# RMS normalisation on one core: statistics one group ahead, the first load in parts, and three large transfers split by partitions

## The chip, the cores and the metric

The kernel runs on one core of one Trainium2 chip. The metric is the device time of one execution in microseconds (us), and lower is better. Quoted times are medians of several executions. The span that a profile shows, from the first to the last instruction, is 1.7 to 1.8 us shorter than the time of the same execution. All timed runs here had a granted clock of 1.0.

## The reference

```python
batch, seq, dim = 16, 1024, 512          # x: float32, gamma: ones
rms = np.sqrt(np.mean(x ** 2, axis=-1, keepdims=True) + 1e-5)
return (x / rms * gamma).astype(np.float32)
```

Each row of 512 numbers is divided by its own root mean square. 33.5 MB are read and 33.5 MB are written, and every row is independent of the others.

## The kernel before

The 16,384 rows are cut into four tiles. A tile gives each of the 128 partitions R = 32 consecutive rows (64 KB), 8.39 MB in all. Three slots in SBUF hold the tiles; tile 3 goes into slot 0 after tile 0 has been stored. SyncE issues all large transfers on one queue.

```python
xv = xf.rearrange("(t p r) d -> t p r d", p=P, r=R)
slots = [const.tile([P, R, D], fp32, name=f"slot{i}") for i in range(3)]

def load(t, slot, r0, r1):
    nc.sync.dma_start(out=slots[slot][:, r0:r1], in_=xv[t][:, r0:r1])

def store(t, slot, r0, r1):
    nc.sync.dma_start(out=ov[t][:, r0:r1], in_=slots[slot][:, r0:r1])

load(0, 0, 0, 16)
load(0, 0, 16, 32)
load(1, 1, 0, 32)
# ... gamma is loaded and spread over the partitions ...

def compute(slot, r0, r1):
    for g in range(r0, r1, G):            # G = 8 rows
        # ... odd groups: Square on ACT into PSUM, tensor_reduce on DVE
        # ... even groups: Square with accum_out on ACT, row by row
        # ... rms = Sqrt(ss / D + eps) on ACT, rstd = reciprocal on DVE
        for r in range(G):                # slot = slot * rstd * gamma on DVE
            nc.vector.scalar_tensor_tensor(...)

compute(0, 0, 8)
store(0, 0, 0, 1); load(2, 2, 0, 16)      # cut: three one-row stores alternate
# ...                                     # with the loads of tile 2
compute(0, 8, 32)
store(0, 0, 3, 32)
# ... tile 1 is stored in two halves of 16 rows, load(3, 0, ...) twice ...
compute(2, 0, 32)
store(2, 2, 0, 32)
compute(0, 0, 16); store(3, 0, 0, 16)
compute(0, 16, 32); store(3, 0, 16, 32)
```

## Time and profile before

| | before |
|---|---|
| time, median (6 runs beside the changed kernel) | 162.05 us |
| span of the profiled execution | 161.0 us |
| DMA queue 1, share of 16 engines' span | 97.4% |
| packet time per DMA engine (sum over 16, divided) | 156.9 us |
| DVE busy | 123.3 us |
| ACT busy | 79.9 us |

The profiled execution of the kernel before took 162.76 us, a little longer than the six timed runs (161.86 to 162.15). So differences between two single traces that are below 1 us are read with care.

These are lines of the profile's page of the kernel before. The rows of digits are busy tenths in 40 slices of about 4 us. Then come the DMA queue, the chain of waits by engine, and two instruction groups (busy us, mean ns, then the engine's idle time before them and what ended it).

```profile
span 161.0 us, 414 instructions
...
DVE  0101909999999509999999999998999999997000
ACT  3007999930490999999500933003998960000000
...
DMA  7999999969798999999699999999999699699993
GB/s 253 399 407 497 399 423 489 521 293 489 326 466 356 466 403 501 460 472 443 297 480 407 415 480 407 407 489 407 407 497 521 277 505 521 269 489 407 407 391 138
...
q1 hardware_dynamic: 2448, 67.11, 97.4%
...
DVE 70%; ACT 12%; DMA 8%; issue 2%; DVEq 0%
...
L78 ACT ACTIVATE sq_scratch<-slot 128x512 f32<-128x512 f32 x64 | 40.1, 627 | 14.4 <-DMA slot<-in_x_dram 13.1
L73 DVE TENSOR_REDUCE ss<-sq 128x4 f32<-128x2048 f32 x16 | 36.1, 2273 | 10.3 <-ACT sq L72 10.2
```

How to read it: the chain of waits names DVE for 70% of the span, yet the DMA row is nearly full from end to end. The queue's own line settles it. The 16 DMA engines spend 97.4% of the span on packets, so no rearrangement of compute can save more than the few per cent that are left. The engines' end times in the trace agree: the last packet ends at 159.65 us, and the rest of the span is completion and the closing barrier.

The windows view gives the rate in three stretches: tile 1's load, tile 0's large store and tile 2's store, each from the last landing of the transfer before it to its own last landing. The last two columns are the DMA share and GB/s.

```profile
22.70:42.40 19.70, 0.00 (x0) 0.00 (x0) 18.45 (x26) 11.08 (x23) 0.00 (x0) 1.00 0.96 407
63.90:82.10 18.20, 0.00 (x0) 0.00 (x0) 18.20 (x29) 14.63 (x37) 0.00 (x0) 1.00 0.97 418
121.30:140.60 19.30, 0.00 (x0) 0.00 (x0) 19.04 (x28) 9.98 (x21) 0.00 (x0) 1.00 1.00 433
```

The engines are full (0.96 to 1.00) and move 407 to 433 GB/s. A view counts a packet where it starts, so a single slice can read above or below the rate of a long window (the slices above, without the first and the last, go from 269 to 521 GB/s); a long window is safer.

The timeline shows when the last store was issued:

```profile
145.87 2.07 DVE L87 SCALAR_TENSOR_TENSOR slot<-slot,rstd,gamma_b 128x512 f32<-128x512 f32 x3
147.97 0.33 SPq L45 DMA_DIRECT2D out_dram<-slot  x1
```

### The profile page before, as it was taken

How to read it: one execution, taken by the hardware profiler on the slowest of the kernel's cores; microseconds unless marked ns; L12 is line 12 of the kernel's file. 1: busy time of each engine (PE TensorE's matmuls, PEld its weight loads, DVE VectorE, ACT ScalarE, POOL GpSimd, SP SyncE). 2: the span in 40 equal slices, each digit the busy share in tenths (PEclk: the TensorE clock that was granted, in tenths of full speed). 3: DMA queues.
4: the chain of work that ended last, by engine and by line, in shares of the span. 5: the costliest groups of instructions: out<-in, count | busy, mean ns of one | idle time of the engine just before them, and what ended most of it. 6: DMA issues, size and time to landing. Idle time of an engine off the chain costs nothing.

```text
span 161.0 us, 414 instructions
## 1 busy us (share of the span) xinstructions
PE 2.0 (1%) x2; PEld 0.5 (0%) x2; DVE 123.3 (77%) x163; ACT 79.9 (50%) x162; POOL 0.2 (0%) x4
## 2 busy tenths in 40 slices
PE   3100000000000000000000000000000000000000
PEld 1000000000000000000000000000000000000000
DVE  0101909999999509999999999998999999997000
ACT  3007999930490999999500933003998960000000
POOL 0000000000000000000000000000000000000000
DMA  7999999969798999999699999999999699699993
GB/s 253 399 407 497 399 423 489 521 293 489 326 466 356 466 403 501 460 472 443 297 480 407 415 480 407 407 489 407 407 497 521 277 505 521 269 489 407 407 391 138
DMA packets 2452, 67.13 MB, mean 417 GB/s; under 512 B 273, under 2 KB 273, under 8 KB 658
## 3 DMA queue, kind: packets, MB, share of 16 engines
q1 hardware_dynamic: 2448, 67.11, 97.4%
q14 instruction: 2, 0.02, 0.0%
q10 hardware_dynamic: 2, 0.00, 0.0%
HBM read 33.56 MB, written 33.55 MB: 417 GB/s over the span
## 4 chain that ended last, share of the span: by engine, by line
DVE 70%; ACT 12%; DMA 8%; issue 2%; DVEq 0%
DVE slot L87 51%; DVE ss L73 18%; DMA slot<-in_x_dram 8%; ACT sq_scratch L78 6%; ACT sq L72 4%; DVE rstd L85 1%; ACT L84 1%; ACT rms L84 1%; DVEq L142 0%
## 5 line engine op out<-in xcount | busy, mean ns | idle before, releaser
L87 DVE SCALAR_TENSOR_TENSOR slot<-slot,rstd,gamma_b 128x512 f32<-128x512 f32 x128 | 85.8, 747 | 0.1
L78 ACT ACTIVATE sq_scratch<-slot 128x512 f32<-128x512 f32 x64 | 40.1, 627 | 14.4 <-DMA slot<-in_x_dram 13.1
L73 DVE TENSOR_REDUCE ss<-sq 128x4 f32<-128x2048 f32 x16 | 36.1, 2273 | 10.3 <-ACT sq L72 10.2
L72 ACT ACTIVATE sq<-slot 128x2048 f32<-128x2048 f32 x16 | 29.8, 1865 | 13.9 <-DVE ss L73 13.9
L84 ACT ACTIVATE rms<-ss,eps_t 128x8 f32<-128x8 f32 x16 | 4.5, 298 | 27.9 <-DVE ss L73 27.7
L78 ACT ACTIVATION_READ_ACCUMULATOR sq_scratch<-slot 128x1 f32 x64 | 12.1, 189 | 0.0
L85 DVE RECIPROCAL rstd<-rms 128x8 f32<-128x8 f32 x16 | 2.9, 193 | 9.8 <-ACT rms L84 9.8
L58 DVE COPY gamma_b<-sq 128x512 f32<-128x512 f32 x1 | 0.7, 691 | 3.6 <-PE sq L56 3.6
L56 PE MATMUL sq<-gamma_row,ones_col 1*128 1x512 f32 x2 | 2.0, 1122 | 2.5 <-DMA gamma_row<-in_gamma_dram 2.5
L78 ACT ACT_TABLE_LOAD x1 | 1.3, 1283 | 1.3 <-PEq L131 1.3
L84 ACT ACT_TABLE_LOAD x1 | 1.3, 1283 | 0.0
L54 DVE MEMSET ones_col<- 1x128 f32 x1 | 0.2, 165 | 0.8 <-PEq L131 0.8
L56 PEld LDWEIGHTS sq<-gamma_row,ones_col 1*128 1x128 f32 x2 | 0.5, 305 | 2.5 <-issue 2.5
L131 POOL MEMSET const-bfloat16-1.0<- 128x1 bf16 x1 | 0.1, 103 | 0.0
L131 POOL MEMSET const-uint8-127<- 128x1 uint8 x1 | 0.1, 103 | 0.0
L131 POOL MEMSET const-float32-1.0<- 128x1 f32 x1 | 0.1, 100 | 0.0
L131 POOL MEMSET const-float32-0.0<- 128x1 f32 x1 | 0.1, 99 | 0.2 <-issue 0.2
L61 DVE MEMSET eps_t<- 128x1 f32 x1 | 0.1, 59 | 0.0
## 6 DMA issues: line engine op xcount, KB each, us to landing
slot<-in_x_dram SPq DMA_DIRECT2D x5, 4096.0 KB, 21.5
out_dram<-slot SPq DMA_DIRECT2D x4, 4096.0 KB, 16.5
out_dram<-slot SPq DMA_DIRECT2D x1, 7424.0 KB, 31.9
slot<-in_x_dram SPq DMA_DIRECT2D x2, 2048.0 KB, 34.2
out_dram<-slot SPq DMA_DIRECT2D x3, 256.0 KB, 22.8
gamma_row<-in_gamma_dram ACTq DMA_DIRECT2D x1, 2.0 KB
slot<-in_x_dram SPq DMA_DIRECT2D x1, 40.8
out_dram<-slot SPq DMA_DIRECT2D x1, 23.5
```

Of the source, the lines that this page charges most:

```text
L54: nc.vector.memset(ones_col, 1.0)
L56: nc.tensor.matmul(gamma_psum[:, 0], ones_col, gamma_row, start=True, stop=True)
L58: nc.vector.tensor_copy(out=gamma_b, in_=gamma_psum[:, 0])
L61: nc.vector.memset(eps_t, eps)
L72: nc.scalar.activation(out=sq, in_=slots[slot][:, g + h : g + h + H, :], func=AF.Square)
L73: nc.vector.tensor_reduce(out=ss[:, h : h + H], in_=sq, axis=mybir.AxisListType.X, op=OP.add)
L78: nc.scalar.activation(out=sq_scratch, in_=slots[slot][:, g + r, :], func=AF.Square, accum_out=ss[:, r : r + 1],)
L84: nc.scalar.activation(out=rms, in_=ss, func=AF.Sqrt, bias=eps_t, scale=1.0 / D)
L85: nc.vector.reciprocal(out=rstd, in_=rms)
L87: nc.vector.scalar_tensor_tensor(out=slots[slot][:, g + r, :], in0=slots[slot][:, g + r, :], scalar=rstd[:, r : r + 1], in1=gamma_b, op0=O ...
L131: nc = _bacc.Bacc("TRN2", target_bir_lowering=False, num_devices=1)
```

## The change

It has three aims. Statistics of a group are computed before the previous group is scaled, so that DVE does not wait for ACT (9.8 us in four waits for `rms` in the kernel before). The first load is cut into 8 and 8 rows, so that ACT starts earlier. And the number of DMAs is raised from 18 to 24, so that the last store falls on the last of the eight DMA semaphores that the trace shows in rotation (numbers 101, 103, 105 to 109 and 99), and the end of the program need not go through further ones. In the kernel before the last store has number 101. To raise the number, three transfers are split, and they are split by partitions.

```diff
+    def load(t, slot, r0, r1, parts=1):
+        for p in range(0, P, P // parts):
+            q = slice(p, p + P // parts)
+            nc.sync.dma_start(out=slots[slot][q, r0:r1], in_=xv[t][q, r0:r1])
 # ... store() in the same way ...
-    load(0, 0, 0, 16)
+    load(0, 0, 0, 8)
+    load(0, 0, 8, 16)
     load(0, 0, 16, 32)
-    load(1, 1, 0, 32)
+    load(1, 1, 0, 32, parts=2)
 # ... compute() becomes row_stats() and apply() ...
-    store(0, 0, 3, 32)
+            store(0, 0, 3, 32, parts=2)
-    store(2, 2, 0, 32)
+            store(2, 2, 0, 32, parts=4)
+    ahead = row_stats(0, 0)
+    for k, (t, g) in enumerate(groups):
+        rstd = ahead
+        if k + 1 < len(groups):
+            tn, gn = groups[k + 1]
+            ahead = row_stats(slot_of[tn], gn)
+        apply(slot_of[t], g, rstd)
+        transfers(t, g)                   # the loads and stores, at the same places
```

More of the change, by code (lines that the diff above doesn't have):

```diff
@@ L39, with store @@
     slots = [const.tile([P, R, D], fp32, name=f"slot{i}") for i in range(3)]
-    def load(t, slot, r0, r1):
-        nc.sync.dma_start(out=slots[slot][:, r0:r1], in_=xv[t][:, r0:r1])
-    def store(t, slot, r0, r1):
-        nc.sync.dma_start(out=ov[t][:, r0:r1], in_=slots[slot][:, r0:r1])
-    load(0, 0, 0, 16)
+    def load(t, slot, r0, r1, parts=1):
+        for p in range(0, P, P // parts):
+            q = slice(p, p + P // parts)
+            nc.sync.dma_start(out=slots[slot][q, r0:r1], in_=xv[t][q, r0:r1])
+    def store(t, slot, r0, r1, parts=1):
+        for p in range(0, P, P // parts):
+            q = slice(p, p + P // parts)
+            nc.sync.dma_start(out=ov[t][q, r0:r1], in_=slots[slot][q, r0:r1])
+    load(0, 0, 0, 8)
+    load(0, 0, 8, 16)
     load(0, 0, 16, 32)
-    load(1, 1, 0, 32)
+    load(1, 1, 0, 32, parts=2)
     gamma_row = const.tile([1, D], fp32)
@@ L62 @@
     sq_scratch = const.tile([P, D], fp32)
-    def compute(slot, r0, r1):
-        for g in range(r0, r1, G):
-            ss = stats.tile([P, G], fp32, name="ss")
-            rms = stats.tile([P, G], fp32, name="rms")
-            rstd = stats.tile([P, G], fp32, name="rstd")
-            if (g // G) % 2:
-                for h in range(0, G, H):
-                    sq = psum.tile([P, H, D], fp32, name="sq")
-                    nc.scalar.activation(out=sq, in_=slots[slot][:, g + h : g + h + H, :], func=AF.Square)
-                    nc.vector.tensor_reduce(
-                        out=ss[:, h : h + H], in_=sq, axis=mybir.AxisListType.X, op=OP.add
-                    )
-            else:
-                for r in range(G):
-                    nc.scalar.activation(
-                        out=sq_scratch,
-                        in_=slots[slot][:, g + r, :],
-                        func=AF.Square,
-                        accum_out=ss[:, r : r + 1],
-                    )
-            nc.scalar.activation(out=rms, in_=ss, func=AF.Sqrt, bias=eps_t, scale=1.0 / D)
-            nc.vector.reciprocal(out=rstd, in_=rms)
-            for r in range(G):
-                nc.vector.scalar_tensor_tensor(
-                    out=slots[slot][:, g + r, :],
-                    in0=slots[slot][:, g + r, :],
-                    scalar=rstd[:, r : r + 1],
-                    in1=gamma_b,
-                    op0=OP.mult,
-                    op1=OP.mult,
-                )
@@ L96, with row_stats @@
-    compute(0, 0, 8)
-    store(0, 0, 0, 1)
-    load(2, 2, 0, 16)
-    store(0, 0, 1, 2)
-    load(2, 2, 16, 24)
-    store(0, 0, 2, 3)
-    load(2, 2, 24, 32)
-    compute(0, 8, 32)
-    store(0, 0, 3, 32)
-    compute(1, 0, 16)
-    store(1, 1, 0, 16)
-    load(3, 0, 0, 16)
-    load(3, 0, 16, 32)
-    compute(1, 16, 32)
-    store(1, 1, 16, 32)
-    compute(2, 0, 32)
-    store(2, 2, 0, 32)
-    compute(0, 0, 16)
-    store(3, 0, 0, 16)
-    compute(0, 16, 32)
-    store(3, 0, 16, 32)
+    def row_stats(slot, g):
+        ss = stats.tile([P, G], fp32, name="ss")
+        rms = stats.tile([P, G], fp32, name="rms")
+        rstd = stats.tile([P, G], fp32, name="rstd")
+        if (g // G) % 2:
+            for h in range(0, G, H):
+                sq = psum.tile([P, H, D], fp32, name="sq")
+                nc.scalar.activation(out=sq, in_=slots[slot][:, g + h : g + h + H, :], func=AF.Square)
+                nc.vector.tensor_reduce(
+                    out=ss[:, h : h + H], in_=sq, axis=mybir.AxisListType.X, op=OP.add
+                )
+        else:
+            for r in range(G):
+                nc.scalar.activation(
+                    out=sq_scratch,
+                    in_=slots[slot][:, g + r, :],
+                    func=AF.Square,
+                    accum_out=ss[:, r : r + 1],
+                )
+        nc.scalar.activation(out=rms, in_=ss, func=AF.Sqrt, bias=eps_t, scale=1.0 / D)
+        nc.vector.reciprocal(out=rstd, in_=rms)
+        return rstd
@@ new lines, in apply, with transfers @@
+    def apply(slot, g, rstd):
+        for r in range(G):
+            nc.vector.scalar_tensor_tensor(
+                out=slots[slot][:, g + r, :],
+                in0=slots[slot][:, g + r, :],
+                scalar=rstd[:, r : r + 1],
+                in1=gamma_b,
+                op0=OP.mult,
+                op1=OP.mult,
+            )
+    groups = [(t, g) for t in range(4) for g in range(0, R, G)]
+    slot_of = [0, 1, 2, 0]
+    def transfers(t, g):
+        if (t, g) == (0, 0):
+            store(0, 0, 0, 1)
+            load(2, 2, 0, 16)
+            store(0, 0, 1, 2)
+            load(2, 2, 16, 24)
+            store(0, 0, 2, 3)
+            load(2, 2, 24, 32)
+        elif (t, g) == (0, 24):
+            store(0, 0, 3, 32, parts=2)
+        elif (t, g) == (1, 8):
+            store(1, 1, 0, 16)
+            load(3, 0, 0, 16)
+            load(3, 0, 16, 32)
+        elif (t, g) == (1, 24):
+            store(1, 1, 16, 32)
+        elif (t, g) == (2, 24):
+            store(2, 2, 0, 32, parts=4)
+        elif (t, g) == (3, 8):
+            store(3, 0, 0, 16)
+        elif (t, g) == (3, 24):
+            store(3, 0, 16, 32)
```

## The prediction

> **What bounds the kernel now.** The DMA engines. The DMA queue view puts queue 1 at 97.4% of 16 engines' span (161.0 us); its packets sum to 156.9 us per engine. DMA is busy without a gap from 2.0 to 148.2 us. It is not busy in three places: 2.0 us at the head; 0.7 us from 148.2, because the last store is issued only at 147.97 (timeline), when the queue has just run dry; and 1.3 us after the last packet (159.65), of which some 0.25 us is SyncE going through four more semaphores after that of the last store. DVE is second: busy 123.3 us, between 24.3 and 147.9 us. The chain of waits names DVE for 70%, but it only just meets the DMA at the end.
>
> **What the change does.**
> 1. First load of 8 rows: half of a 4 MB load that landed at 12.95, so about 7.5 us. ACT starts 5 us earlier. Off the DMA path: same bytes.
> 2. Statistics one group ahead: the same work; DVE's waits on ACT (5.4 us near 60, 3.8 us near 24) shrink. With (1) DVE should end 8 to 12 us earlier, and the last store is queued in time. Gain on the critical path: the 0.7 us hole only.
> 3. Last store on the last semaphore: about 0.25 us at the end.
> Gains together: 1 us, 0.6%. Over 2% is not to be had, since the bytes stay.
> 4. The price is the partition split: tile 1's load and tile 0's store as 2 x 64 partitions, tile 2's store as 4 x 32. [...] The trace of before has no such transfer and can't confirm it. In before a 65,536-byte packet took 2.418 us, 8 per engine: 19.3 us for 8.4 MB. At half rate: tile 1's load +19.3, tile 0's store (8 x 2.192) +17.5, tile 2's store +19.3: +56 us, an estimate, all on the critical path, as the queue is never empty.
>
> **Prediction.** [...] 162.1 - 1.0 + 56 = 217 us. If not: 161.1. If only loads or only stores suffer: 180 or 198. The first is likelier: 215 us, range 160.8 to 219. Faster by over 2%: 0.02; within 2%: 0.34; slower by over 2%: 0.64.
>
> **What would show it.** Packets of 65,536 bytes of the split transfers take about 4.8 us each (right) or 2.42 (wrong). GB/s of the slices: about 215 during tile 1's load and the stores of tiles 0 and 2. Tile 1's load lands near 61 us instead of 42.4. DMA share stays over 95%: engines "busy" but slow. DVE's busy time stays near 123 us. For the gains: ACT's first Square at 7 to 8 us; no DMA hole before the last store; no further semaphore waits between the last landing and the end barrier.
>
> **What would make it wrong.** [...]

The sum came to 217 us: 162.1 - 1.0 + 56. What is cut under 4 is the ground on which the rate of the split transfers was halved, with its figures; before the sum the condition is cut, that the rate halves, and "if not" is its opposite. No trace had shown the half rate; the runs below measure it (200 GB/s against 407 in tile 1's load). The last paragraph named what would leave both halves at full rate, 161 us, and said that engines that drift apart would give part of the rate back. No trace shows the mechanisms that it named.

## The result, and the profile after

The changed kernel takes 220.74 us (219.90 to 221.53, 6 runs) against 162.05 us (161.86 to 162.15, 6 runs). The ratio is 1.3625, 95% interval 1.3586 to 1.3664. Ratios here are the mean time of one kernel's runs over that of the other's of the same rounds, so not quite the ratio of the medians quoted. Executions over 1.5% slower than the fastest of the same kernel are left out of the means.

The same parts of the page, for the changed kernel (a slice is 5.5 us here):

```profile
span 219.7 us, 425 instructions
...
DVE  1029999930008099999999991087999900000000
ACT  2595880000049999760930000499910000000000
...
DMA  7999999899989999889986999999999899969981
GB/s 263 430 453 513 251 191 191 191 191 191 191 334 407 418 422 439 173 173 324 195 173 286 436 346 430 436 400 424 477 227 191 191 286 215 215 221 436 442 376 78
...
q1 hardware_dynamic: 2672, 67.11, 97.2%
...
another core or an unknown queue 26%; DVE 24%; ACT 16%; DMA 13%; issue 1%; DVEq 0%; SPq 0%; ACTq 0%
...
L82 ACT ACTIVATE sq_scratch<-slot 128x512 f32<-128x512 f32 x64 | 40.0, 626 | 55.8 <-DMA slot<-in_x_dram 54.5
L77 DVE TENSOR_REDUCE ss<-sq 128x4 f32<-128x2048 f32 x16 | 36.2, 2279 | 40.5 <-ACT sq L76 40.2
```

Every engine does the work it did before: DVE 123.1 us, ACT 80.1 us, 67.13 MB. The queue is as full as before (97.2%), but in three stretches the GB/s row falls to about half while the DMA row mostly stays at 8 to 9 tenths. A busy share says that packets are in flight, not that bytes move quickly: the windows below have shares of 0.93 to 1.00 at 200 to 231 GB/s. The chain of waits has a new entry, "another core or an unknown queue", 26%. It is not another core: its first piece ends at 63.48 us, where the trace has the last landing of tile 1's load. That half of the load was issued at 2.70 us, and the view did not tie a landing to an issue so long before it.

The windows view of the same three transfers, again from last landing to last landing:

```profile
22.80:63.50 40.70, 0.00 (x0) 0.00 (x0) 23.03 (x32) 9.77 (x20) 0.00 (x0) 1.00 0.93 200
85.30:119.70 34.40, 0.00 (x0) 0.00 (x0) 34.40 (x47) 16.85 (x37) 0.00 (x0) 1.00 1.00 226
160.10:199.50 39.40, 0.00 (x0) 0.00 (x0) 15.90 (x22) 0.30 (x1) 0.00 (x0) 1.00 0.97 231
```

The three stretches sum to 114.5 us where they were 57.2 us. That difference, 57.3 us, is nearly all of the 58.7 us by which the two profiled spans differ.

The trace's packet records show it packet by packet. This table is worked out from them; times are us for one packet, minimum / median / mean / maximum.

| packets | before | after |
|---|---|---|
| tile 1's load, 65,536 B, 128 packets | 2.42 / 2.42 / 2.47 / 3.03 | 4.52 / 5.12 / 5.04 / 5.13 |
| tile 0's store, 59,392 B, 128 packets | 2.19 / 2.19 / 2.20 / 2.56 | 2.19 / 4.63 / 4.21 / 5.79 |
| tile 2's store, 65,536 B, 128 packets | 2.42 / 2.42 / 2.42 / 2.46 | 2.42 / 5.11 / 4.69 / 5.91 |

There is one more thing to see, which no row of the page shows. The trace has 16 landings for each large transfer by one DMA, read here as one from each of the 16 DMA engines. In the kernel before, the 16 landings of the last store lie between 158.87 and 159.99 us (mean 159.02). In the changed kernel they lie between 210.24 and 218.85 us (mean 215.52), 8.6 us apart. The loads keep the engines together (62.85 to 63.48 for tile 1's load); the split stores drive them apart: 3.6 us after tile 0's store, 8.6 us after tile 2's.

The timeline shows that the intended parts of the change worked. This line is ACT's first Square, at 7.93 us instead of 12.97:

```profile
7.93 0.63 ACT L82 ACTIVATE sq_scratch<-slot 128x512 f32<-128x512 f32 x1 [5.37 <-DMA slot<-in_x_dram]
```

The last store was issued at 176.03 us, 33 us before the store ahead of it had landed (209.19), so the queue no longer runs dry. From the last landing to the end of the span there are 0.82 us (218.85 to 219.67) instead of 0.99 (159.99 to 160.98), because SyncE goes through no further semaphore where it went through three (at 160.05, 160.11 and 160.18 us): the last semaphore is worth 0.17 us.

### The profile page after: what moved, and what is told of

It is laid out like the page before. It is cut to its first block, busy times and chain, and to the rows that moved or that the text cites. A ratio compares the mean times of both kernels' runs of the same rounds, so it can differ in the third digit from the quotient of the medians.

```text
span 219.7 us, 425 instructions
## 1 busy us (share of the span) xinstructions
PE 2.0 (1%) x2; PEld 0.5 (0%) x2; DVE 123.1 (56%) x163; ACT 80.1 (36%) x162; POOL 0.2 (0%) x4
## 2 busy tenths in 40 slices
DMA packets 2677, 67.13 MB, mean 306 GB/s; under 512 B 370, under 2 KB 370, under 8 KB 755
## 3 DMA queue, kind: packets, MB, share of 16 engines
q1 hardware_dynamic: 2672, 67.11, 97.2%
## 4 chain that ended last, share of the span: by engine, by line
another core or an unknown queue 26%; DVE 24%; ACT 16%; DMA 13%; issue 1%; DVEq 0%; SPq 0%; ACTq 0%
DVE slot L94 19%; DMA slot<-in_x_dram 13%; ACT sq_scratch L82 9%; ACT sq L76 6%; DVE ss L77 5%; DVE rstd L89 1%; ACT rms L88 1%; DVEq L162 0%; SPq L49 0%; SPq L44 0%; ACTq L82 0%
```

## The experiments

The theory: a transfer confined to 64 or 32 neighbouring partitions of SBUF runs, for that reason, at half the rate (200 GB/s against 407 in tile 1's load). In the expectations the figures that follow "[...]" are this theory's. The rivals: (A) more and smaller DMAs, or their semaphores, cost the time; (B) the new order of the computation delays the queue; (C) 64 rows on 16 engines are slow wherever they lie; (D) the HBM side, where a part of a tile lies in half of the tile's stretch, is slow. All results were correct against the reference. Where the text speaks of packet records or landings, these are worked out from the trace itself, as no view lists them one by one.

### The same number of DMAs, split over rows

```diff
-        for p in range(0, P, P // parts):
-            q = slice(p, p + P // parts)
-            nc.sync.dma_start(out=slots[slot][q, r0:r1], in_=xv[t][q, r0:r1])
+        for r in range(r0, r1, n):                  # n = ceil((r1 - r0) / parts)
+            e = min(r + n, r1)
+            nc.sync.dma_start(out=slots[slot][:, r:e], in_=xv[t][:, r:e])
 # ... store() in the same way ...
```

> The changed kernel with every split made over the rows of a partition instead of over the partitions: as many DMAs (24), the same semaphores, each DMA over all 128 partitions. [...] the loss goes, 160.5 to 161.5 us, packets of 32,768 bytes at 1.21 us. Rival A (more and smaller DMAs, or their semaphores, cost the time): about 220 us again.

Measured: 163.28 us (162.52 to 164.05), ratio to the kernel before 1.0071 (1.0046 to 1.0097). The loss is gone with as many DMAs and the same rotation of semaphores, so rival A falls. It missed my 160.5 to 161.5: this version is 0.7% slower than the kernel before. In its trace the last landings lie between 158.41 and 161.14 us: fifteen engines are done by 158.92, and one, 2.2 us later, ends the kernel. What makes it trail was not tested.

### No splits at all

```diff
-    load(1, 1, 0, 32, parts=2)          # and parts=2, parts=4 of the stores
+    load(1, 1, 0, 32)
```

> The changed kernel without any of the three splits: statistics ahead and first load in parts remain. [...] 160.8 to 161.8 us; against the row-split kernel it shows what the last semaphore is worth, 0.1 to 0.3 us. Rival B (statistics one group ahead delays the stores, and so the DMA queue): clearly over 165 us.

Measured: 162.64 us (162.49 to 163.77), ratio 1.0040 (1.0014 to 1.0065). Rival B falls: the new order costs half a microsecond at most. But the gain I had promised is not there either: the time is above my 160.8 to 161.8. As for the last semaphore, the two times cannot show it, because the trailing engine differs by more between the two kernels (last landings at 161.14 and 159.84 us). The ends of the traces do: from the last landing to the end there are 1.05 us here and 0.82 with the rows split, 0.23 us, within my 0.1 to 0.3.

### The same splits, but every second or fourth partition

```diff
-        for p in range(0, P, P // parts):
-            q = slice(p, p + P // parts)
+        for p in range(parts):
+            q = slice(p, P, parts)
```

> The changed kernel with the same number of partitions per part, 64 or 32, and the same packet sizes, but every second (fourth) partition instead of neighbouring ones[...]. [...] about 161 us, packets of 65,536 bytes near 2.42 us. Rival C (64 rows over 16 engines are slow in themselves, 4 packets an engine, wherever they lie): about 220 us and packets near 5 us.

Measured: 162.15 us (162.11 to 162.32), ratio 1.0001 (0.9985 to 1.0016). Number of DMAs, partitions per DMA, packets per engine and packet sizes are those of the changed kernel; only which partitions form a part differs, and the whole loss vanishes. (It is 162 and not my 161 because the gain of 1 us is missing here too.) By the packet records tile 1's load has packets of 2.42 us in the median. Rival C falls. Its page, to be held against the changed kernel's:

```profile
span 160.4 us, 425 instructions
...
DMA  6999999969799999997999999999999799899993
GB/s 197 441 417 507 400 392 523 523 262 523 327 394 412 454 431 511 459 474 326 400 425 482 392 425 490 392 400 507 400 515 458 343 507 425 368 392 441 466 400 139
...
q1 hardware_dynamic: 2672, 67.11, 97.8%
```

The windows of the same three transfers, as for the other two kernels:

```profile
22.50:42.20 19.70, 0.00 (x0) 0.00 (x0) 19.66 (x28) 9.77 (x20) 0.00 (x0) 1.00 0.94 396
64.30:81.80 17.50, 0.00 (x0) 0.00 (x0) 17.50 (x27) 10.16 (x26) 0.00 (x0) 1.00 0.97 421
120.90:140.20 19.30, 0.00 (x0) 0.00 (x0) 19.30 (x27) 5.37 (x15) 0.00 (x0) 1.00 1.00 431
```

The three long dips to between 170 and 230 GB/s are gone at the same packet count (2,677 and 2,676 in all by the two pages).

### The splits alone, on the kernel before

```diff
-load(1, 1, 0, 32)
+load(1, 1, 0, 32, parts=2)               # likewise store(0, 0, 3, 32) in 2, store(2, 2, 0, 32) in 4
```

> The kernel before with nothing but the partition splits of the three transfers. [...] 218 to 221 us, so the split explains all of the loss. Rival B: near 162 us, or part of the way.

Measured: 221.85 us (220.65 to 223.11), ratio 1.3681 (1.3635 to 1.3727). It is 0.9 us above my range and 1.1 us above the changed kernel, with overlapping runs. The splits by neighbouring partitions explain all of the loss, from the other direction.

### One split at a time

Each is the changed kernel with one of the three splits kept:

```diff
 load(1, 1, 0, 32, parts=2)               # load1_only keeps this one
-store(0, 0, 3, 32, parts=2)              # store0_only keeps this one instead
+store(0, 0, 3, 32)
-store(2, 2, 0, 32, parts=4)              # store2_only keeps this one instead
+store(2, 2, 0, 32)
```

> The changed kernel with only the load of tile 1 in two halves of 64 neighbouring partitions. [...] from the packets of the changed kernel (5.05 us against 2.42, 8 per engine): 20 to 21 us over the kernel without splits (162.6), so 182.5 to 184; landings of the 16 engines stay within 1 us of each other[...]. If the loss came from the stores only: 162.6.

> Only the store of tile 0 (29 rows) in two halves. [...] packets of 59,392 bytes at 4.2 us on average against 2.19, so 16 us over the kernel without splits, 178 to 180. In the changed kernel the engines leave this store 3.5 us apart (116.1 to 119.7); if that spread is carried to the end rather than evened out, it adds 1 to 2 us more.

> Only the store of tile 2 in four parts of 32 partitions. [...] packets at 4.69 us on average against 2.42, so 18 us over the kernel without splits by the mean engine, and 2 to 3 us more because the engines leave it apart and the slowest ends the kernel: 181 to 184, with last landings of the 16 engines spread over 6 us or more. The three separate losses should add up to that of the changed kernel (58) within 3 us.

| kept | time, us | over the kernel without splits (162.64) | packet mean, us | last 16 landings spread |
|---|---|---|---|---|
| tile 1's load in 2 | 183.53 (183.19 to 183.69) | 20.9 | 5.02 | 1.8 us |
| tile 0's store in 2 | 180.88 (180.41 to 181.09) | 18.2 | 4.21 | 3.3 us |
| tile 2's store in 4 | 182.82 (182.60 to 183.01) | 20.2 | 4.82 | 5.3 us |
| all three (the change) | 220.74 | 58.1 | see above | 8.6 us |

The three add up to 59.3 us, the change has 58.1, so they behave as separate losses on one full queue. (The kernel without splits ran in another set of rounds; the kernel before was 162.12 us in that set and 162.19 in this one.) Loads and stores both lose. Tile 0's store came out 0.9 us above my range, as I had said it would if the spread was carried to the end, and the landings show that it was: 2.9 us apart when that store landed, 3.3 us apart at the end. For tile 2's store the time is as expected, but the spread of 5.3 us is less than the 6 or more that I had said. For the load, the profile's window from the last landing before it shows the half rate by itself:

```profile
22.80:63.10 40.30, 0.00 (x0) 0.00 (x0) 23.02 (x32) 9.77 (x20) 0.00 (x0) 1.00 0.93 201
```

### SBUF or HBM: the two sides crossed

Neighbouring partitions hold neighbouring rows of HBM, so the experiments so far changed both sides together. RMS normalisation does not care which partition holds which rows. So tile 1 alone was split, its load and both stores, once with halves of SBUF and alternating 64 KB rows of HBM, once the other way round.

```diff
+    def sides(t):
+        if t == 1:   # partitions, and the rows of HBM that they hold
+            return [(slice(0, 64), slice(0, 128, 2)), (slice(64, 128), slice(1, 128, 2))]
+        return [(slice(0, P), slice(0, P))]
+    # the counterpart: [(slice(0, 128, 2), slice(0, 64)), (slice(1, 128, 2), slice(64, 128))]
```

> Only tile 1 is split, its load and its two stores, into partitions 0 to 63 and 64 to 127; but the lower half holds the even 64 KB rows of HBM and the upper half the odd ones, so that each part spreads over the tile's whole stretch of HBM. [...] still slow, load packets near 5 us, and 20 us for the load plus 16 to 20 for the stores: 198 to 204. Rival (half a tile's stretch of HBM is slow): 162 to 163.

> The counterpart: tile 1's load and stores split into even and odd partitions, but each part lies in one half of the tile's stretch of HBM. [...] no loss, 162 to 163, load packets at 2.42 us. Rival (HBM side): 198 to 204.

Measured: 200.49 us (199.29 to 201.24), ratio 1.2341, with SBUF halves and spread HBM rows; 162.16 us (161.80 to 162.32), ratio 0.9987 (0.9962 to 1.0012), with spread partitions and HBM halves. The load's windows, first of the one and then of the other:

```profile
22.90:63.30 40.40, 0.00 (x0) 0.00 (x0) 22.94 (x32) 9.77 (x20) 0.00 (x0) 1.00 0.93 200
```

```profile
22.60:42.20 19.60, 0.00 (x0) 0.00 (x0) 19.57 (x28) 9.77 (x20) 0.00 (x0) 1.00 0.94 401
```

Rival D falls, for halves of one tile's stretch of HBM. The loss belongs to the partitions of SBUF.

### Four parts of 32 or two of 64

```diff
-            store(2, 2, 0, 32, parts=4)
+            store(2, 2, 0, 32, parts=2)          # no other split
```

> The store of tile 2 in two halves of 64 partitions instead of four parts of 32. [...] about the same loss as with four parts, 180 to 184. [...]

Measured: 182.88 us (182.32 to 183.70) against 182.82 us with four parts. 32 neighbouring partitions are no worse than 64.

### Two queues

```diff
-    load(1, 1, 0, 32)
+    nc.sync.dma_start(out=slots[1][0 : P // 2], in_=xv[1][0 : P // 2])
     nc.scalar.dma_start(out=gamma_row, in_=gamma.unsqueeze(0))
+    nc.scalar.dma_start(out=slots[1][P // 2 : P], in_=xv[1][P // 2 : P])
```

> Tile 1's load in two halves, the lower issued by SyncE as before, the upper by ScalarE's queue at the start[...]. [...] If the engines stay in step[...]: near the one-queue split, 180 to 184.

Measured: 186.26 us (184.25 to 188.92). Two of the four runs, 187.11 and 188.92, count as slow, although their clock is 1.0 too; what slowed them is not known. The fast ones took 184.25 and 185.41 us against 183.53 with one queue: no gain, rather 0.7 and 1.9 us worse, and just above my 180 to 184. The upper half, moved beside the first 16 rows of tile 0 on the other queue, had not gained rate. These 16 rows and the half had all landed at 33.81 us; with one queue the 16 rows had landed at 12.78 us, and a half took 20.1 us (42.97 to 63.11), together 32.9. So the two side by side cost 0.9 us more than one after the other, and in the profiled runs that is nearly all of the difference (spans of 182.46 and 181.40). The first group arrived at 28.9 us instead of 7.9, so all computation was late, and by the packet records most DMA engines stood idle from 169.7 to 170.8 us, before the last store. But this hole did not cost the time: the last landing of the store before it was already 1.07 us later than with one queue (171.72 and 170.65), and the last landing of all 1.06 us (181.39 and 180.33). Both halves starting at the same time was not tried.

### The kernel before, profiled again

> The kernel before, unchanged, for a second profile of it: does the 0.7 us hole in the DMA before the last store, on which my forecast of a 1 us gain rested, appear in another execution? If yes: span 160 to 161 with the DMA idle near 148.2. If not, the gain was never there to be had.

Measured: 162.12 us, span 160.3 us. The hole is there again: by the packet records fewer than eight engines are busy from 148.34 to 148.59 us. So it is real, and yet removing it gained nothing, which needs an explanation (next section).

## Why the prediction was right or wrong

- **What bounds the kernel: right.** The queue is 97% full before and after.
- **The price of the split: right in kind. That neighbouring partitions of SBUF cost the time is confirmed by removal, by addition and by the crossed experiment.** The half rate, an assumption in the forecast, is what the runs measure: neighbouring halves run at 200 GB/s against 407, and 32 partitions do as well as 64 (182.82 and 182.88 us). A 64-row DMA still has 16 landings: the trace of the changed kernel has 368 four-byte writes on SyncE's queue, 16 for each of its 23 DMAs, as the kernel before has 272 for its 17.
- **The range: wrong.** I said 160.8 to 219 and the time is 220.74. My own sum was 217; I then stated 215, pulled towards the outcomes that I held less likely, and left only 2 us above the sum. The step that failed is the sum, 162.1 - 1.0 + 56: two of its terms were mis-sized. Against the version with alternating partitions (162.15 us) the split costs 58.6 us and not 56, and without it the change gains nothing and not 1 us.
- **First mis-sized term: "+56 us", three packet times doubled.** It is a sum for the mean engine, and for the mean engine it was good: packet time per engine went from 156.87 us (the version with alternating partitions) to 213.42, +56.55. Inside it, partly by luck, two errors cancel. The load is worse than double: 8 packets x (5.04 - 2.47) = 20.6 us instead of 19.3; 65,536 B in 5.12 us are 12.8 GB/s for one engine, less than half of the 27.1 that it moves in the load without a split (2.418 us). The stores are better than double by the mean packet (4.21 and 4.69 us instead of 4.38 and 4.84), because some packets ran at full speed: the minimum is still 2.19 and 2.42. But the kernel ends with its slowest engine, not with the mean one. In the version with alternating partitions the last landing of the last store is 1.04 us after the mean of the 16 (159.56 and 158.52), in the changed kernel 3.33 us (218.85 and 215.52). That is 2.29 us more. The mean landing itself moved by 57.00 us (from 158.52 to 215.52), and 57.00 + 2.29 is the whole 59.29 us between the two spans (219.67 and 160.39). I had named drifting engines as something that would give rate back. They gave back a little in the stores and took more at the end.
- **Second mis-sized term: "Gains together: 1 us".** All of the change without neighbouring partitions measures 162.15 us, a gain of nothing. The 0.17 us of the last semaphore are visible at the end of the trace; I had said 0.25 for four further semaphores, and there were three. The other part, "the 0.7 us hole only", was not on the critical path. I read it from the sum of the engines again, and even there the packet records give an idle time of 0.4 us for the mean engine. In the kernel before, the slowest engine landed tile 3's first half at 150.31 us and its second at 159.99, 9.68 us later; in the kernel without splits, which has no hole, it is also 9.68 us (150.16 to 159.84). In the second profile of the kernel before it is 9.69 us (149.66 to 159.35). The records do not name the engine, but they agree: one engine ends a packet at 148.76 us and starts the next at once. For the engine that ends the kernel there never was a hole: the others waited, and it used the wait to catch up. The spread of the landings fell from 1.82 to 1.12 us across the hole.
- **Statistics one group ahead, first load in parts: right that they work and that they lie off the DMA path.** ACT starts at 7.93 us. In the kernel without splits the last store is issued at 142.62 us instead of 147.97, 5.4 us earlier; I had said 8 to 12.
- **The checks that I listed:** packets of 4.8 us came out at 5.12 us in the median for the load; windows of 215 GB/s at 200, 226 and 231; tile 1's load near 61 us at 63.48; DMA share over 95% at 97.2%; DVE busy near 123 us at 123.1; after the last landing no further semaphore wait, as forecast.

Open: why a transfer of neighbouring partitions of SBUF runs at half the rate; no run shows the mechanism, and a part made of blocks from both halves of the partitions was not tried. Open too: why the packets of a split load take nearly equally long (4.52 to 5.13 us) and those of a split store do not (2.42 to 5.91), and why the landings lie 0.7 to 2.7 us apart at the end even where nothing is split into neighbouring partitions. No version beat the kernel before.

## What to carry to other kernels

When a transfer must be cut, cut it over the free dimension or over alternating partitions, not into blocks of neighbouring partitions (32 or 64 in these runs): here that choice alone was the difference between 162 and 221 us. A DMA row that is full says nothing of the rate (shares of 0.93 to 1.00 stood beside 200 to 231 GB/s here, and beside 407 to 433), so read GB/s beside it, over a window as long as the transfer. This kernel, bound by 16 parallel engines, ended with the slowest, 3.33 us after their mean, so look at each engine's own landing before counting a gap of the others as time to be won.
